# Queries and keys of the second attention and of retention projected with columns in the rows, their rotary step over partition rows with SBUF transfers and GpSimd

## The chip, the cores and the metric

The kernel runs on one core of a Trainium2 chip. A core has five engines that work side by side and meet through semaphores: TensorE (PE) multiplies matrices and transposes, VectorE (DVE) and ScalarE (ACT) work elementwise on SBUF and PSUM, GpSimd (POOL) does elementwise work on SBUF, and SyncE (SP) issues transfers. The metric is the device time of one execution in microseconds (us), lower is better. Before the change it is 839.24 us, the median of three runs between 838.96 and 839.48.

## What is computed

A decoder trunk of two layers over 256 tokens of width 1024. Each layer normalises, projects with one wide matrix `w_in`, runs three token mixers on parts of the projection, merges them behind gates, and adds a squared-ReLU MLP. Cut to what matters here:

```python
def apply_rope(x, cos, sin):
    half = x.shape[-1] // 2
    x1, x2 = x[..., :half], x[..., half:]
    return jnp.concatenate([x1 * c - x2 * s, x1 * s + x2 * c], axis=-1)

p = rms_norm(x, attn_norm[l]) @ w_in
(cq, ckv, k_rope, mq, mk, mv, rq, rk, rv, rg, g_mla, g_moba, g_ret) = split(p)
o_mla  = mla_branch(...)        # first attention, 8 heads
o_moba = moba_branch(mq, mk, mv)  # second attention, 8 heads of 64, the first 16 of each turned
o_ret  = retention_branch(rq, rk, rv, rg)  # 4 heads of 64, all 64 turned
merged = (sigmoid(g_mla) * (o_mla @ w_branch_mla)
          + sigmoid(g_moba) * (o_moba @ w_branch_moba)
          + sigmoid(g_ret) * (o_ret @ w_branch_ret))
x = x + merged @ w_out
x = x + square(relu(rms_norm(x, mlp_norm[l]) @ w_up)) @ w_down
```

With 256 tokens there is one MoBA block, so the second attention is causal attention over all tokens. In the retention, scores are multiplied by a fixed decay instead of a softmax. "Rotary step", or rope, is `apply_rope`.

## The kernel before

**Numbers.** Everything is float32. A weight block comes from memory as `raw` (up to 128 x 1024, 512 KB, on SP's queue), ACT rounds it to a high part `whi` and DVE subtracts to get the low part `wlo` (lines 191 and 193). There are 4 `raw` buffers and 6 each of `whi` and `wlo`. The normalised activations `xs` are held in the same two parts, with the channels in the partition rows and both parts side by side. A product then is three matmuls (`three`, lines 211 to 214): high by high, high by low, low by high.

**Order.** The matrix work of a layer is a list of units, `prog`; `at(slot(key, i), step)` hangs a step (transposes, scores, softmax) behind unit `i` of the projection `key`. A scheduler with due times orders the instructions of each engine within what this list, the buffers and the data allow; between `tc.manual_schedule` marks PE's order is as written. Projections run in the order b0 (the MLA's compressed q and kv), mq, mk, the MLA's own up projections between the units of mv, gmla, gmoba, bmla, rqk, rv, rg, bmoba, gret, bret, wout, and then the MLP.

**Tokens in the rows.** `project` (line 324) takes two accumulators in PSUM, one for each 128 tokens, and walks over four weight blocks of two channel groups each: 48 matmuls over 512 columns for a projection of 512. The tag `acc` has 4 banks, the tag `misc` another 4. `moba_done` and `ret_done` (lines 624 and 799) evict with an ACT copy that multiplies by the reciprocal norm of the token (`xn.col`), and for mq, mk and rqk `rope` (line 359) follows: two products and a sum and a difference on DVE.

**Turning.** The scores need channels in the rows. `moba_turn` (line 776) transposes mq and mk, 8 transposes of 128x128 for each of 4 pairs of heads into a bank `pqk`; `ret_turn` (line 812) does the same for rqk into `prt`. `copied_pair` (line 391) copies the bank to `qkT` on ACT. The scores of four heads then run together (`together`, line 381): `moba_scores` (line 785) at gmoba0's second unit and GAP = 8 units later, `ret_scores` (line 822) at rg's first unit. `in_a_row` (line 373) writes PE's order by hand for the values of the heads before and the scores of the next ones.

**The start.** In layer 0 the projections b0 and mq run together, channel group by channel group as x arrives (`start`, line 635). In layer 1 b0 runs in two turns, one for each 128 tokens, while the last MLP results of layer 0 are turned and added (`before`, line 1092). `c_norms` (line 594) then squares x, sums and calls `stats`; `xn.square` adds up on DVE in the attention norm and on GpSimd in the MLP norm.

**The MLP's up projection** (line 987) already gives channels in the rows: 8 matmuls over 512 columns with `whi` as the stationary operand and both parts of xs as the moving one, then 8 over 256 with `wlo`; lines 1010 and 1011 add the halves.

Of the kernel before, what the change touches and what calls it, by code (L numbers as in the profile page):

```python
# [14 lines left out]
P = 128  # L15
D = 1024
S = 256
# [17 lines left out]
C_MQ, C_MK, C_MV = range(416, 928), range(928, 1440), range(1440, 1952)  # L35
# [7 lines left out]
]  # L43
C_KV = [P * h + o + i for o in (0, NOPE) for h in range(MLA_H) for i in range(64)]


def weight_plan():

    plan = []

    def block(key, name, kt, cols, per):
        for j in range(0, kt, per):
            plan.append(((*key, j // per), name, (j, per), cols))

    def span(c, n):
        return range(c, c + n)

    for l in range(L):
        if l == 0:

            for i in range(2):
                plan.append(((l, "mq", i), "w_in", (0, 1), span(C_MQ.start + 256 * i, 256)))
            plan.append(((l, "b0", 0), "w_in", (0, 1), C_MLA))
            for k in range(1, KD):
                plan.append(((l, "b0mq", k), "w_in", (k, 1), range(0, 928)))
# [50 lines left out]
K_COS_RT = K_SIN_MB + NT * 8  # L116
K_SIN_RT = K_COS_RT + NT * 32
K_DEC = K_SIN_RT + NT * 32
K_END = K_DEC + RT_H * 3 * P

# [8 lines left out]
def trunk(ctx: ExitStack, tc: tile.TileContext, gx, wts, consts, gfin, gn, xtok, out):  # L129
# [16 lines left out]
    DEC = cp.tile([P, K_END - K_DEC], F32, name="DEC")  # L146
# [90 lines left out]
    class Normed:  # L237


        def __init__(self, g0, adds=nc.vector):  # L240
            self.g0, self.adds = g0, adds
            self.parts = [t4(f"xs{i}").rearrange("p (k two) s -> p k two s", two=2) for i in range(KD // 2)]
            self.sums = []
# [12 lines left out]
        def square(self, n):  # L256
            if n == 0:
                self.sum = sb.tile([P, S], F32, name="sqsum", bufs=1)
                nc.scalar.activation(self.sum, chunk(n), AF.Square)
            else:  # L260
                sq = sb.tile([P, S], F32, name="xsq", bufs=2)
                nc.scalar.activation(sq, chunk(n), AF.Square)
                self.adds.tensor_add(self.sum, self.sum, sq)
# [94 lines left out]

    def rope(xv, c0, s0, t, n, h, w=None):

        w = w or n
        cos = K[:, c0 + t * w : c0 + t * w + n][:, None, None, :].to_broadcast([P, h, 2, n])
        sin = K[:, s0 + t * w : s0 + t * w + n][:, None, None, :].to_broadcast([P, h, 2, n])
        a = sb.tile([P, 512], F32, name="ropea", bufs=1)
        b = sb.tile([P, 512], F32, name="ropeb", bufs=1)
        av = a[:, : 2 * h * n].rearrange("p (h two n) -> p h two n", h=h, two=2)
        bv = b[:, : 2 * h * n].rearrange("p (h two n) -> p h two n", h=h, two=2)
        nc.vector.tensor_mul(av, xv, cos)
        nc.vector.tensor_mul(bv, xv, sin)
        nc.vector.tensor_sub(xv[:, :, 0, :], av[:, :, 0, :], bv[:, :, 1, :])  # L370
        nc.vector.tensor_add(xv[:, :, 1, :], av[:, :, 1, :], bv[:, :, 0, :])
# [18 lines left out]

    def copied_pair(pt):

        o = sb.tile([P, 2 * S], F32, name="qkT", bufs=4)
        nc.scalar.copy(o, pt)
        return o[:, 0:S], o[:, S:]
# [150 lines left out]
    xn = Normed(G_ATT)  # L546
# [11 lines left out]
    begin((0, "mk", 0))  # L558
# [28 lines left out]
    def layer(l, xn, before):  # L587
# [36 lines left out]
        def moba_done(key):  # L624
            def done(accs):
                dst = mqkv[key] = [w2k(key) for _ in range(NT)]
                for t in range(NT):
                    nc.scalar.activation(dst[t], accs[t], AF.Copy, scale=xn.col[t])
                    if key != "mv":
                        xv = dst[t].rearrange("p (h d) -> p h d", h=MB_H)[:, :, 0:16]  # L630
                        rope(xv.rearrange("p h (two n) -> p h two n", two=2), K_COS_MB, K_SIN_MB, t, 8, MB_H)
# [30 lines left out]

        if l:
            project(l, "mq", xn, 512, moba_done("mq"))
# [9 lines left out]
        project(l, "mk", xn, 512, moba_done("mk"))  # L674
# [82 lines left out]
        if l == 0:  # L757
            at(slot("gmla1", 0), lambda: tc.keep_in_program_order(nc.sync.dma_start(DEC, consts[:, K_DEC:])))
# [13 lines left out]
        first = slot("gmoba0", 1)  # L772
        at(first, lambda: omobaT.extend((t4("omobah"), t4("omobal"))))
        qkT = {}

        def moba_turn(i):
            pt = misc_tile("pqk")
            for a, key in enumerate(("mq", "mk")):
                for t in range(NT):
                    nc.tensor.transpose(  # L780
                        pt[:, (2 * a + t) * P : (2 * a + t + 1) * P], mqkv[key][t][:, P * i : P * i + P], ident
                    )
            qkT[i] = copied_pair(pt)

        def moba_scores(h0):
# [3 lines left out]
                [(banks[2 * i : 2 * i + 2], *qkT[h0 // 2 + i]) for i in range(2)],  # L789
# [3 lines left out]
        for i in range(4):  # L793
            at(first + 4 * (i // 2) - 3 + i % 2, lambda i=i: moba_turn(i))
# [4 lines left out]
        def ret_done(key):  # L799
            def done(accs):  # L800
                dst = rqkv[key] = [w2k(key) for _ in range(NT)]
                for t in range(NT):
                    nc.scalar.activation(dst[t], accs[t], AF.Copy, scale=xn.col[t])
                    if key == "rqk":
                        xv = dst[t].rearrange("p (h two n) -> p h two n", h=2 * RT_H, two=2)
                        rope(xv, K_COS_RT, K_SIN_RT, t, 32, 2 * RT_H)

            return done

        rT, or_ps, aT, rg, oret = [], [], {}, {}, []  # L810

        def ret_turn(i):
            pt = misc_tile("prt")
            for a in range(2):
                for t in range(NT):
                    nc.tensor.transpose(
                        pt[:, (2 * a + t) * P : (2 * a + t + 1) * P],
                        rqkv["rqk"][t][:, 256 * a + P * i : 256 * a + P * i + P], ident,
                    )
            rT.append(copied_pair(pt))  # L820

        def ret_scores():
# [3 lines left out]
                [(banks[2 * i : 2 * i + 2], rT[i][1], rT[i][0]) for i in (1, 0)],  # L826
# [58 lines left out]
        project(l, "rqk", xn, 512, ret_done("rqk"))  # L885
# [43 lines left out]
        for i in range(2):  # L929
            at(slot("rv", 1 + i), lambda i=i: ret_turn(i))  # L930
# [35 lines left out]
        def wout_first():  # L966
            xm.append(Normed(G_MLP + KD * l, nc.gpsimd))
# [101 lines left out]
        if not last:  # L1069
            xn = Normed(G_ATT + KD * (l + 1))  # L1070
# [83 lines left out]
def constants():  # L1154
# [14 lines left out]
    for c, s, dim, theta in (  # L1169
        (K_COS_MLA, K_SIN_MLA, ROPE, 500000.0),  # L1170
        (K_COS_MB, K_SIN_MB, MB_D // 4, 500000.0),
        (K_COS_RT, K_SIN_RT, RT_K, 10000.0),
    ):
        n = dim // 2
        inv = f(1.0) / (f(theta) ** (np.arange(0, dim, 2, dtype=f) / f(dim)))
        ang = np.arange(S, dtype=f)[:, None] * inv[None, :].astype(f)
        two = 2 if c == K_COS_MLA else 1
        w = two * n
        for t in range(NT):
            K[:, c + t * w : c + t * w + w] = np.tile(np.cos(ang[P * t : P * t + P]), two)  # L1180
            K[:, s + t * w : s + t * w + w] = np.tile(np.sin(ang[P * t : P * t + P]), two)
    return K
# [44 lines left out]
```

## Time and profile before

| | before |
|---|---|
| Device time, median of 3 runs | 839.24 us (838.96 to 839.48) |
| Profiled execution, its own time | 839.34 us |
| Its span, first to last instruction | 837.5 us |
| Granted TensorE clock, mean | 0.999 |
| Queries and keys transposed, `pqk` and `prt` | 32 and 16 transposes |
| Transfers on SP's queue | 151 MB in all, mean 180 GB/s |

The times come from runs without the profiler; the profile describes one further execution, whose span is 1.8 us shorter than its own time. An engine's busy time is the union of its instructions; PE's matmuls are pipelined, so records overlap, and a matmul's length is more than what it adds. In a row of groups stand line, engine, operation, names and shapes, count, then the duration (least, median and most in ns, and first and last start) or the busy time and mean. "idle before <-releaser" is the time that the engine waited just before and what ended the wait.

### The profile page before, as it was taken

Reading aid. Unit: us, or ns where it says so; the run is one execution under the profiler, and the core shown is the slowest. Engines: PE = TensorE matmul, PEld = TensorE weight load, DVE = VectorE, ACT = ScalarE, POOL = GpSimd, SP = SyncE. Lnnn points to the kernel's source line nnn. Section 1 sums busy time; section 2 is a strip of 40 time slices with the busy share of each in tenths; the row PEclk is TensorE's granted clock in tenths of the full one; section 3 lists DMA queues with packets and bytes.
Section 4 is the critical chain, followed back from the end, with each engine's and each line's share of the span. In section 5 each row is a group of like instructions: output and inputs, shape, how many; then the busy total and the mean of one; then the engine's idle time right before and its main releaser. Section 6 shows DMA issues by size and latency. Waiting matters only on the chain.

```text
span 837.5 us, 11975 instructions
## 1 busy us (share of the span) xinstructions
PE 830.7 (99%) x4342; PEld 702.9 (84%) x4342; DVE 577.0 (69%) x1088; ACT 490.0 (59%) x860; POOL 42.0 (5%) x45
## 2 busy tenths in 40 slices
PE   9999999999999999999999999999999999999997
PEld 7888788888888888888888888888888888888886
DVE  6887567595787666656589765766968775556663
ACT  7857566445555555555677576744555555555552
POOL 0100000040030000000000000001201200000000
PEclk9999999999999999999999999999999999999999
DMA  9865454536456656666367544564565666666641
GB/s 345 271 201 188 144 166 146 175 125 213 141 180 228 193 193 189 195 187 189 114 202 223 173 143 151 151 182 149 157 199 163 213 179 193 199 189 192 196 129 51
DMA packets 43115, 151.09 MB, mean 180 GB/s; under 512 B 4912, under 2 KB 5936, under 8 KB 43056
## 3 DMA queue, kind: packets, MB, share of 16 engines
q1 hardware_dynamic: 42480, 149.66, 56.7%
q8 instruction: 34, 0.56, 0.3%
q10 hardware_dynamic: 576, 0.67, 0.2%
q14 instruction: 25, 0.20, 0.1%
HBM read 149.26 MB, written 1.05 MB: 179 GB/s over the span
## 4 chain that ended last, share of the span: by engine, by line
PE 99%; ACT 0%; DVE 0%; issue 0%; DVEq 0%
PE acc L212 20%; PE acc L213 20%; PE acc L214 20%; PE pup L1002 13%; PE pup L1004 7%; PE acc L952 5%; PE ps_s L763 1%; PE ps_pt L429 1%; PE po L456 1%; PE ps_s L389 1%; PE acc L656 1%; PE acc L657 0%; PE acc L659 0%; PE warm L567 0%; PE po L458 0%; PE pqk L780 0%
## 5 line engine op out<-in xcount | busy, mean ns | idle before, releaser
L193 DVE TENSOR_TENSOR wlo<-raw,whi 128x1024 fp32r<-128x1024 f32 (+4 forms) x287 | 339.2, 1188 | 205.8 <-ACT whi L191 152.1
L191 ACT ACTIVATE whi<-raw 128x1024 fp32r<-128x1024 f32 (+4 forms) x287 | 292.0, 1023 | 178.8 <-PE acc L214 101.9
L212 PE MATMUL acc<-whi,xs 128*128 128x512 f32 (+1 forms) x384 | 152.0, 398 | 0.0
L213 PE MATMUL acc<-wlo,xs 128*128 128x512 f32 (+1 forms) x384 | 150.6, 392 | 0.0
L214 PE MATMUL acc<-whi,xs 128*128 128x512 f32 (+1 forms) x384 | 150.1, 392 | 0.0
L1002 PE MATMUL pup<-xs,whi 128*128 128x512 f32 x496 | 121.5, 390 | 0.0
L1002 PEld LDWEIGHTS pup<-xs,whi 128*128 128x128 f32 x496 | 91.9, 188 | 18.3
L212 PE MATMUL acc<-whi,sq 128*128 128x512 f32 x256 | 100.1, 391 | 0.0
L213 PE MATMUL acc<-wlo,sq 128*128 128x512 f32 x256 | 99.9, 390 | 0.0
L214 PE MATMUL acc<-whi,sq 128*128 128x512 f32 x256 | 98.8, 389 | 0.0
L214 PEld LDWEIGHTS acc<-whi,xs 128*128 128x128 f32 x384 | 72.1, 188 | 14.3
L212 PEld LDWEIGHTS acc<-whi,xs 128*128 128x128 f32 x384 | 72.1, 188 | 14.2 <-issue 0.7
L213 PEld LDWEIGHTS acc<-wlo,xs 128*128 128x128 f32 x384 | 72.2, 188 | 13.7 <-issue 0.3
L1004 PE MATMUL pup<-xs,wlo 128*128 128x256 f32 x496 | 68.8, 283 | 0.0
L1004 PEld LDWEIGHTS pup<-xs,wlo 128*128 128x128 f32 x496 | 65.7, 191 | 3.1
L1013 ACT ACTIVATE relu<-relu 128x256 f32<-128x256 f32 x64 | 25.5, 408 | 54.1 <-DVE relu L1012 54.1
L214 PEld LDWEIGHTS acc<-whi,sq 128*128 128x128 f32 x256 | 48.1, 188 | 10.2
L212 PEld LDWEIGHTS acc<-whi,sq 128*128 128x128 f32 x256 | 48.2, 188 | 9.2
L213 PEld LDWEIGHTS acc<-wlo,sq 128*128 128x128 f32 x256 | 48.2, 188 | 8.9
L418 ACT ACTIVATE prob<-prob,smx 128x128 f32<-128x128 f32 x64 | 28.4, 445 | 20.1 <-DVE smx L415 20.0
L952 PE MATMUL acc<-mT,whi 128*128 128x512 f32 (+1 forms) x144 | 35.3, 372 | 0.0
L1010 ACT COPY relu<-pup 128x256 f32<-128x256 f32 x62 | 22.3, 365 | 16.0 <-PE pup L1004 15.2
(246 smaller groups left out, 1006.0 us busy)
## 6 DMA issues: line engine op xcount, KB each, us to landing
raw<-wts SPq DMA_DIRECT2D x264, 512.0 KB, 4.1
raw<-wts SPq DMA_DIRECT2D x6, 464.0 KB, 8.0
raw<-wts SPq DMA_DIRECT2D x4, 416.0 KB, 3.3
xrow<-xtok SPq DMA_DIRECT2D x4, 256.0 KB, 8.0
gn<-gn SPq DMA_DIRECT2D x2, 512.0 KB, 4.7
raw<-wts SPq DMA_DIRECT2D x3, 256.0 KB, 4.1
DEC<-consts SPq DMA_DIRECT2D x1, 768.0 KB, 6.0
y<-y SPq DMA_DIRECT2D x2, 352.0 KB, 2.6
```

The source lines that it names most:

```text
L191: nc.scalar.activation(hi[:, cs], raw[:, cs], AF.Copy)
L193: nc.vector.tensor_sub(lo[:, cs], raw[:, cs], hi[:, cs].bitcast(F32))
L212: nc.tensor.matmul(o, ah, bh, start=start, stop=False)
L213: nc.tensor.matmul(o, ah, bl, start=False, stop=False)
L214: nc.tensor.matmul(o, al, bh, start=False, stop=stop)
L389: nc.tensor.matmul(bank[:, o], a[rows, sa], b[rows, sb_], start=True, stop=True)
L418: nc.scalar.activation(p[:, a:b], p[:, a:b], AF.Exp, bias=m[:, 2 + i : 3 + i], scale=scale, accum_out=m[:, 4 + i : 5 + i])
L952: nc.tensor.matmul(o, a, b, start=half == 0 and i == 0, stop=4 * half + n == KD and i == len(jobs) - 1)
L1002: nc.tensor.matmul(u, w, xm.both(k), start=k == 0, stop=False)
L1004: nc.tensor.matmul(u[:, 0:S], w, xm.k(k)[0], start=False, stop=k == KD - 1)
L1010: nc.scalar.copy(s, u[:, S : 2 * S])
L1013: nc.scalar.activation(s, s, AF.Square)
```

## The change

mq (in layer 1), mk and rqk are projected like the MLP's up projection, so that channels lie in the rows without a transpose. Each is four units of 128 columns (`project_turned`), each with one accumulator bank and one weight block; pairs of units make a tile `qkraw` of 128 x 512. It is not multiplied by the norm: the rope's tables are (`tables`, on GpSimd). The rope then needs the other half of each head, which lies in other partition rows. `rope_turned` fetches it with four transfers of 32 x 512 from `qkraw` to `qkoth` on SP's queue, and makes two products and a sum; in MoBA all of it on GpSimd, in the retention one product on GpSimd and the rest on DVE. The columns of mq and mk are put in such an order that the turned 16 of each head lie in rows that a transfer of 32 rows exchanges. In layer 0 mq stays with tokens in the rows and is transposed, four banks' worth reduced to two.

The joint MoBA scores and all that hangs on them move from the second unit of gmoba0 to that of gmoba1, four units later. In layer 1 three of the seven additions of squares (n = 1 to 3) are done by GpSimd. The tables come with one more transfer of 512 KB (`TAB`) in layer 0; the constants `K` are 128 columns shorter.

```diff
+    def turned(key, cols):
+        for n in range(4):
+            block((*key, n), "w_in", KD, cols[P * n : P * n + P], KD)
...
             block((l, "b0"), "w_in", KD, C_MLA, 2)
-            block((l, "mq"), "w_in", KD, C_MQ, 2)
-        block((l, "mk"), "w_in", KD, C_MK, 2)
+            turned((l, "mq"), C_MQ)
+        turned((l, "mk"), C_MK)
...
-        block((l, "rqk"), "w_in", KD, C_RQK, 2)
+        turned((l, "rqk"), C_RQK)
...
-                self.adds.tensor_add(self.sum, self.sum, sq)
+                (nc.gpsimd if n < self.on_pool else nc.vector).tensor_add(self.sum, self.sum, sq)
...
+    def project_turned(l, key, xn, done):
+        pair = []
+        def unit(n):
+            wh, wl = load_w(l, key, n, 0)
+            acc = acc_tile()
+            for k in range(KD):
+                nc.tensor.matmul(acc, wh[:, k, :], xn.both(k), start=k == 0, stop=False)
+            for k in range(KD):
+                nc.tensor.matmul(acc[:, 0:S], wl[:, k, :], xn.k(k)[0], start=False, stop=k == KD - 1)
+            if n % 2 == 0:
+                pair.append(w2k("qkraw"))
+            second = sb.tile([P, S], F32, name="second", tag="relu", bufs=3)
+            nc.scalar.copy(second, acc[:, S : 2 * S])
+            nc.vector.tensor_add(halves(pair[-1])[:, n % 2, :], acc[:, 0:S], second)
+            if n % 2:
+                done(n // 2, pair[-1])
+        for n in range(4):
+            prog.append(((key, n), lambda n=n: unit(n)))
+
+    def tables(xn, kind):
+        o = sb.tile([P, 2 * S], F32, name="tab", bufs=1)
+        for i in range(2):
+            cs = slice((2 * kind + i) * S, (2 * kind + i) * S + S)
+            nc.gpsimd.tensor_mul(o[:, S * i : S * i + S], TAB[:, cs], xn.row)
+        return o
+
+    def rope_turned(raw, tab, engine):
+        other = w2k("qkoth")
+        for quarter in range(4):
+            a, b = 32 * quarter, 32 * (quarter ^ 1)
+            nc.sync.dma_start(other[a : a + 32, :], raw[b : b + 32, :])
+        o = sb.tile([P, 2 * S], F32, name="qkT", bufs=4)
+        cos, sin = (tab[:, S * i : S * i + S][:, None, :].to_broadcast([P, 2, S]) for i in range(2))
+        engine.tensor_mul(halves(o), halves(raw), cos)
+        nc.gpsimd.tensor_mul(halves(other), halves(other), sin)
+        engine.tensor_add(o, o, other)
+        return halves(o)
...
+        def moba_rope(key, i):
+            if "tab" not in mqkv:
+                mqkv["tab"] = tables(xn, 0)
+            qkT[key][i] = rope_turned(mqkv[key, i], mqkv["tab"], nc.gpsimd)
...
+        for i in range(2):
+            if l:
+                at(slot("mk", 1 + 2 * i), lambda i=i: moba_rope("mq", i))
+            at(slot("gmla0", 1 + 2 * i), lambda i=i: moba_rope("mk", i))
...
-        first = slot("gmoba0", 1)
+        first = slot("gmoba1", 1)
...
-        for i in range(4):
-            at(first + 4 * (i // 2) - 3 + i % 2, lambda i=i: moba_turn(i))
+        if l == 0:
+            for i in range(2):
+                at(first + 4 * i - 3, lambda i=i: moba_turn(i))
...
+        def ret_pair(i, raw):
+            if i == 0:
+                rqkv["tab"] = tables(xn, 1)
+            rT.append(rope_turned(raw, rqkv["tab"], nc.vector))
...
-        project(l, "rqk", xn, 512, ret_done("rqk"))
+        project_turned(l, "rqk", xn, ret_pair)
...
-        for i in range(2):
-            at(slot("rv", 1 + i), lambda i=i: ret_turn(i))
...
-            xm.append(Normed(G_MLP + KD * l, nc.gpsimd))
+            xm.append(Normed(G_MLP + KD * l, KD))
...
-            xn = Normed(G_ATT + KD * (l + 1))
+            xn = Normed(G_ATT + KD * (l + 1), 4)
```

More of the change, by code (lines that the diff above doesn't have):

```diff
@@ L34 @@
 C_MLA = range(0, 416)
[L35 removed]
+C_MV = range(1440, 1952)
 C_RQK, C_RV, C_RG = range(1952, 2464), range(2464, 2976), 2976
@@ L43 @@
 ]
+C_MQ, C_MK = (
+    [c + 64 * h + i for h in range(8) for i in (*range(8), *range(16, 40), *range(8, 16), *range(40, 64))] for c in (416, 928)
+)
 C_KV = [P * h + o + i for o in (0, NOPE) for h in range(MLA_H) for i in range(64)]
@@ L363, in rope @@
         sin = K[:, s0 + t * w : s0 + t * w + n][:, None, None, :].to_broadcast([P, h, 2, n])
-        a = sb.tile([P, 512], F32, name="ropea", bufs=1)
-        b = sb.tile([P, 512], F32, name="ropeb", bufs=1)
+        a = sb.tile([P, S], F32, name="ropea", bufs=1)
+        b = sb.tile([P, S], F32, name="ropeb", bufs=1)
         av = a[:, : 2 * h * n].rearrange("p (h two n) -> p h two n", h=h, two=2)
@@ L661, in start, with moba_pair, done @@
                 moba_done("mq")(mq)
+        qkT = {"mq": {}, "mk": {}}
+        def moba_pair(key):
+            def done(i, raw):
+                mqkv[key, i] = raw
+            return done
+        def moba_rope(key, i):
+            if "tab" not in mqkv:
+                mqkv["tab"] = tables(xn, 0)
+            qkT[key][i] = rope_turned(mqkv[key, i], mqkv["tab"], nc.gpsimd)
         if l:
-            project(l, "mq", xn, 512, moba_done("mq"))
+            project_turned(l, "mq", xn, moba_pair("mq"))
             at(slot("mq", 1), c_norms)
@@ L771, in layer @@
         branch(l, "bmla", omlaT, th_mla, merged)
-        first = slot("gmoba0", 1)
+        first = slot("gmoba1", 1)
         at(first, lambda: omobaT.extend((t4("omobah"), t4("omobal"))))
-        qkT = {}
         def moba_turn(i):
-            pt = misc_tile("pqk")
-            for a, key in enumerate(("mq", "mk")):
+            pt = misc_tile("pq")
+            for a in range(2):
                 for t in range(NT):
+                    k = 2 * i + a
                     nc.tensor.transpose(
-                        pt[:, (2 * a + t) * P : (2 * a + t + 1) * P], mqkv[key][t][:, P * i : P * i + P], ident
+                        pt[:, (2 * a + t) * P : (2 * a + t + 1) * P], mqkv["mq"][t][:, P * k : P * k + P], ident
                     )
-            qkT[i] = copied_pair(pt)
+            o = sb.tile([P, 2 * S], F32, name="qkT", bufs=4)
+            nc.scalar.copy(o, pt)
+            qkT["mq"][i] = halves(o)
         def moba_scores(h0):
@@ L788, in moba_scores @@
                 ((slice(0, P), slice(0, P), slice(0, P)), (slice(P, 3 * P), slice(P, S), slice(0, S))),
-                [(banks[2 * i : 2 * i + 2], *qkT[h0 // 2 + i]) for i in range(2)],
+                [(banks[2 * i : 2 * i + 2], *(qkT[key][h0 // 4][:, i, :] for key in ("mq", "mk"))) for i in range(2)],
             )
             return banks
-        for i in range(4):
-            at(first + 4 * (i // 2) - 3 + i % 2, lambda i=i: moba_turn(i))
+        if l == 0:
+            for i in range(2):
+                at(first + 4 * i - 3, lambda i=i: moba_turn(i))
         moba_last = attention(omobaT, None, lambda: mqkv["mv"], MB_D**-0.5, first, moba_scores, mla_last)
@@ L825, in ret_scores @@
                 ((slice(0, S), slice(0, P), slice(0, S)), (slice(S, 3 * P), slice(P, S), slice(P, S))),
-                [(banks[2 * i : 2 * i + 2], rT[i][1], rT[i][0]) for i in (1, 0)],
+                [(banks[2 * i : 2 * i + 2], rT[1][:, i, :], rT[0][:, i, :]) for i in (1, 0)],
             )
@@ L1181, in constants @@
             K[:, s + t * w : s + t * w + w] = np.tile(np.sin(ang[P * t : P * t + P]), two)
+    for j, (dim, theta) in enumerate(((MB_D // 4, 500000.0), (RT_K, 10000.0))):
+        ang = angles(dim, theta).T
+        n = dim // 2
+        c = K_TURNED + 2 * S * j
+        K[:, c : c + S] = 1.0
+        for quarter in range(4):
+            rows = slice(32 * quarter, 32 * quarter + n)
+            K[rows, c : c + S] = np.cos(ang)
+            K[rows, c + S : c + 2 * S] = np.sin(ang) * (1 if quarter % 2 else -1)
     return K
```

63 lines of the change are left out of this document (22 added, 41 removed).

## The prediction, made before the changed kernel was run

> **What bounds the kernel now.** I read the busy times of the engines first, then the chain of waits, then the windows by stage.
>
> ```profile
> PE 830.7 (99%) x4342; PEld 702.9 (84%) x4342; DVE 577.0 (69%) x1088; ACT 490.0 (59%) x860; POOL 42.0 (5%) x45
> ...
> PE 99%; ACT 0%; DVE 0%; issue 0%; DVEq 0%
> ```
>
> TensorE is busy for 830.7 of 837.5 us, and the chain that ended last lies on it for 99%. The windows (microseconds; busy time and count of PE, of its weight loads, of DVE, ACT and POOL; granted clock; DMA share; GB/s) show where the missing 6.8 us are:
>
> ```profile
> 0.00:40.00 40.00, 39.23 (x180) 32.53 (x181) 29.81 (x75) 31.44 (x61) 3.54 (x12) 1.00 0.88 311
> ...
> 450.00:480.00 30.00, 30.00 (x163) 25.81 (x162) 25.45 (x54) 19.32 (x31) 0.00 (x0) 1.00 0.57 178
> ...
> 820.00:837.50 17.50, 11.61 (x54) 9.37 (x53) 5.35 (x11) 4.76 (x13) 1.10 (x2) 0.94 0.15 60
> ```
>
> At the start 0.77 us are lost and at the end 5.89; between them PE hardly stops, and the clock is granted in full. The change touches neither end. So between the ends only two things count: what PE's own instructions cost, and whether anything new makes PE wait. DVE, at 25.45 of 30 us early in the second layer, is the engine with the least room behind it.
>
> **The price of PE's instructions.** The length of a matmul's record isn't its price, since records overlap; the price is the distance from one to the next, which the chain of waits gives as the time of a run:
>
> ```profile
> 90.67 0.44 PE pqk L780 x4
> ...
> 153.41 0.66 PE prt L816 x6
> ...
> 278.74 0.23 PE acc L214
> 278.97 3.63 PE pup L1002 x16
> 282.60 1.91 PE pup L1004 x16
> ...
> 418.00 0.19 PE acc L212
> ```
>
> A transpose of 128x128 costs 0.44/4 = 0.11 us, a matmul over 512 columns 3.63/16 = 0.227, one over 256 columns 1.91/16 = 0.119, one over 416 columns 0.19.
>
> **What goes.** The transposes of mq, mk and rqk:
>
> ```profile
> L780 PE MATMUL pqk<-K,mq x16: 270/272/273, 90.5 to 520.7; 128*128 128x128 f32 x16
> ...
> L780 PE MATMUL pqk<-K,mk x16: 272/272/273, 90.7 to 520.9; 128*128 128x128 f32 x16
> ...
> L816 PE MATMUL prt<-K,rqk x16: 270/272/273, 148.9 to 567.0; 128*128 128x128 f32 x16
> ```
>
> These are 48. Eight remain: layer 0 makes mq with tokens in the rows as before, and its turn, now called pq, takes 2 banks of 4. Forty at 0.11 us are -4.4 us on the path.
>
> **What PE pays for it.** A projection of 512 columns now costs 48 matmuls over 512 columns, 48 x 0.227 = 10.90 us. Turned, each of four units has 8 over 512 columns (the high weights with both parts of xs side by side) and 8 over 256 (the low weights): 32 x 0.227 + 32 x 0.119 = 11.08 us. That is the same form as the MLP's up projection, lines 1002 and 1004, whose rows I use. Five projections change (mk and rqk of layer 0, mq, mk and rqk of layer 1): 5 x 0.18 = +0.9 us. The scores have the same shapes as before. Without a new wait the sum is -3.5 us.
>
> **Work on the other engines.**
>
> ```profile
> L394 ACT COPY qkT<-pqk x8: 558/578/595, 91.1 to 523.3; 128x512 f32<-128x512 f32 x8
> ...
> L1010 ACT COPY relu<-pup x62: 346/364/377, 248.1 to 817.9; 128x256 f32<-128x256 f32 x62
> L1011 DVE TENSOR_TENSOR relu<-pup,relu x62: 414/418/425, 249.5 to 818.3; 128x256 f32<-128x256 f32 x62
> ...
> L368 DVE TENSOR_TENSOR ropea<-rqk,K x4: 685/689/693, 142.3 to 558.7; 128x512 f32<-128x512 f32 x4
> ...
> L370 DVE TENSOR_TENSOR rqk<-ropea,ropeb x4: 418/422/426, 143.6 to 561.0; 128x256 f32<-128x256 f32 x4
> ...
> L803 ACT ACTIVATE rqk<-acc,ms x4: 690/690/692, 141.6 to 555.5; 128x512 f32<-128x512 f32 x4
> ...
> L263 POOL TENSOR_TENSOR sqsum<-sqsum,xsq 128x256 f32<-128x256 f32 x14 | 16.0, 1142 | 117.3 <-ACT xsq L262 117.2
> L895 POOL TENSOR_TENSOR rgb<-rg,gn 128x512 f32<-128x512 f32 x4 | 5.1, 1284 | 273.4 <-DVE rg L894 273.4
> ```
>
> Each turned unit is evicted by an ACT copy (0.364) and a DVE add (0.418), 20 of each: 7.3 and 8.4 us. ACT loses ten evictions of 0.69 and ten qkT copies of 0.578, 12.7 us; DVE loses rqk's rope, 4 x (2 x 0.689 + 2 x 0.422) = 8.9 us, and the shorter ropes of mq and mk, and gains 8 operations of 0.689 for retention's turned rope. Neither has more work in sum than now; only their order can cost PE something. GpSimd's part is new: for each of 6 MoBA pairs two products and a sum over 512 columns, for each of 4 retention pairs one product, 22 at 1.28 us by the rgb row, and 8 table products of 256 columns and three additions of layer 1's squares at 1.14 (DVE does the latter in 0.42). That is some 40 us over both layers; for MoBA the cover is the distance from projection to scores, tens of microseconds, and the joint rows move from gmoba0's second unit to gmoba1's. I put them at nothing.
>
> The 40 transfers stand in SP's queue among the weights, so each delays the blocks behind it by its issue, and those by what it waits for itself.
>
> ```profile
> 171.46 0.33 SPq L176 DMA_DIRECT2D raw<-wts  x1
> ```
>
> ```profile
> L193 DVE TENSOR_TENSOR wlo<-raw,whi 128x1024 fp32r<-128x1024 f32 (+4 forms) x287 | 339.2, 1188 | 205.8 <-ACT whi L191 152.1
> L191 ACT ACTIVATE whi<-raw 128x1024 fp32r<-128x1024 f32 (+4 forms) x287 | 292.0, 1023 | 178.8 <-PE acc L214 101.9
> ```
>
> ACT and DVE split weights ahead of PE and idle because PE still holds the six buffers (101.9 us of ACT's idle time). A block lasts PE 12 x 0.227 = 2.73 us, so in the steady stages they are three to five blocks ahead, 8 to 14 us. Four issues, 4 x 0.33 = 1.3 us, vanish in that. If the cover were gone, as at a stage where blocks arrive just in time, ten groups of 1.3 us would be 13 us.
>
> **Where I expect a new wait: the start of layer 1.** Timeline of before there:
>
> ```profile
> 423.19 0.63 PE L212 MATMUL acc<-whi,xs 128*128 128x512 f32 x2
> ...
> 425.30 3.06 DVE L263 TENSOR_TENSOR sqsum<-sqsum,xsq 128x256 f32<-128x256 f32 x6
> 429.16 4.63 DVE L193 TENSOR_TENSOR wlo<-raw,whi 128x1024 fp32r<-128x1024 f32 x4 [0.79 <-ACT whi L191]
> ...
> 434.97 1.06 ACT L191 ACTIVATE whi<-raw 128x1024 fp32r<-128x1024 f32 x1 [2.45 <-DMA raw<-wts]
> ```
>
> Transfers (KB each, median us from issue to landing):
>
> ```profile
> raw<-wts SPq DMA_DIRECT2D x264, 512.0 KB, 4.1
> ...
> GX<-gx SPq DMA_DIRECT2D x1, 11.0 KB, 6.2
> ```
>
> The projections have four acc banks. In the changed order b0's two halves hold two of them until the statistics, mq's units 0 and 1 the others, and unit 2 must wait until unit 0's bank is evicted. From 423.19 PE has 24 matmuls over 416 columns (4.56) and 13 of unit 0 and unit 1's high part (2.95), then unit 0's low part (0.95): 431.65. Unit 1's last three high and its low ones take it to 433.3, the sums of squares to 433.5. Unit 0's eviction stands on ACT behind the high part of the third mk block, and its DVE add behind the low part. That block's buffer comes free when mq's third block is split, which waits for b0's first whi buffer (PE, near 424.8) and for ACT: some 426.4 to 427.7 us on DVE. A transfer then lands 4.1 us later, near 432 (the 2.45 us that ACT idles before 434.97 is this same kind of wait). whi to 433.0, the copy to 433.4, wlo (4.63/4 = 1.16) to 434.3, the add to 434.7: PE stands from 433.5 to 434.7, 1.2 us. Bounds: none if the block lands by 430.8; 2.4 us if one wlo more (1.16) gets in ahead of the add. I take 1.2, by the landing that is the median of 264 such blocks.
>
> The next bank (unit 1's) comes about 1 us before PE asks. In layer 0 the evictions of mk lie before no such queue.
>
> **The sum** for the profiled execution: 839.34 (span 837.5, 1.8 around it) - 4.4 + 0.9 + 1.2 = 837.0 us; it stood 0.1 above the median of the three runs, which changes nothing at this size.
>
> **Retention, the tightest new chain.** From the end of rqk's second unit (T), DVE's add comes at T+1.2 to T+1.7 after a wlo block. SP issues four transfers until T+3.0; a weight block is issued just ahead of them. At 4.1 us they land by T+7.1, GpSimd's product ends at T+8.4, DVE's sum at T+9.1. This sum stands in the middle of the second MoBA group's softmax on DVE, which today runs like this, first maximum to last scaling:
>
> ```profile
> 124.27 0.28 DVE L409 CUSTOM_DVE_ANT_0 prob<-ps_s,K 128x128 f32<-128x128 f32 x1
> ...
> 129.43 0.55 DVE L423 TENSOR_SCALAR prob<-prob,smx 128x128 f32<-128x128 f32 x2
> ```
>
> The second head's scaling, queued behind the sum, ends by T+9.7; PE transposes that head at T+10.4 (1.9 for values and scores, 2 x 2.77 for units 2 and 3, 2.73 for rv's first unit, 0.33). Pair 1 is evicted by about T+14, lands by T+19.2, is summed by T+21.2 and used at T+22.3. So both waits just miss PE, by 0.7 and 1.1 us; every microsecond of landing beyond about 5 is paid, in each layer. I take nothing for it.
>
> **Rivals.**
> (1) No bank wait: the third mk block lands early. For: ACT has slack there. Against: the 2.45 us idle. 839.3 - 3.5 = 835.8.
> (2) GpSimd gets in DVE's way. Its reads beside DVE's:
>
> ```profile
> 169.07 1.28 POOL L895 TENSOR_TENSOR rgb<-rg,gn 128x512 f32<-128x512 f32 x1 [133.02 <-DVE rg L894]
> ...
> 169.30 2.13 DVE L193 TENSOR_TENSOR wlo<-raw,whi 128x1024 fp32r<-128x1024 f32 x1 [0.36 <-ACT whi L191]
> 170.43 2.16 POOL L896 TENSOR_TENSOR rg<-rg,gn 128x512 f32<-128x512 f32 x1
> ```
>
> A wlo that takes 1.16 to 1.23 us took 2.13 here, 0.9 more, and the next GpSimd product 2.16 for 1.28. Layer 1 puts 12 such products (4 pairs x 3) between 445 and 490; at 0.9 each DVE loses up to 10.8 us where its idle time is 4.55 of 30, against 8 to 14 us of slack. Up to 2.5 us would reach PE: about 837 to 839.5, nearest to 838.5. The Trainium skill has a rule for it (SBUF — State Buffer, "Who interferes with whom"): a Vector instruction with two SBUF inputs and a GpSimd instruction that reads SBUF take turns at a shared port, the later one blocked until the earlier ends. The rows agree: the wlo ends 1.08 us after the first product, as if begun then. By that rule alone a product could cost DVE its whole 1.28 us, 15.4 for the twelve, and this rival would end near 840.
> (3) Slower: the small transfers queue behind weight blocks. Place: retention in both layers. If the last lands 6.2 us after its issue (the 11 KB row, taken where DMA is 88% busy; here it is about 55%), pair 0's sum ends at T+11.2 and the second head is 1.4 late; pair 1 then follows some 1.9 late. About 3 us a layer: 837.0 + 6 = 843. It costs from 5 us of landing on, and eats the gain from about 5.8 on.
> (4) The change doesn't shorten PE at all, if 256-column matmuls cost more than 0.119 in this order. The pup row, with the same loads and shapes, speaks against it.
>
> **How the numbers follow.** The forecast with its neighbourhood (836.3 to 838) has 0.42, rival 1 0.15, rival 2 0.23, rival 3 0.18, rival 4 0.02. What a measurement of this kernel can tell from no change is 0.2%, 1.7 us: faster is below 837.56, slower above 840.92. Faster takes nearly all of rival 1, most of the forecast's part and a little of rival 2: 0.58. Same takes the forecast's upper tail and most of rival 2: 0.22. Slower: rival 3 and the end of rival 2: 0.20. The likeliest case alone ranges from 835.8 to 838.5; the range for 8 in 10 goes from 835.4 to 842, taking in the lower half of rival 3.
>
> **What would show it.** PE's busy time falls by about 3.5 us to 827, with 40 fewer transposes. In the chain of waits one break of 1 to 2 us near 433, released by DVE's add. No break at the joint scores of MoBA. The transfers of 64 KB land in 3 to 5 us; above 5 the retention scores or the transposes of the second head show PE idle. A wlo beside GpSimd's products lasts 2 us. Wrong would be: PE idle spread over 445 to 490 (rival 2), or a busy time of PE that doesn't fall.

## The result, and the profile after

| | before | after |
|---|---|---|
| Device time, median of 22 runs | 839.17 us (838.80 to 839.69) | 837.92 us (837.43 to 839.04) |
| Ratio of after to before | | 0.9986 (95% interval 0.9980 to 0.9993) |
| Profiled execution, its own time | 839.34 us | 837.58 us |
| Its span | 837.5 us | 835.8 us |

The change takes 1.25 us away, 0.14%: a gain whose interval leaves out 1, and which is smaller than the 0.2% that the prediction called measurable. The profiled execution gained 1.76 us; it lies 0.34 below its own median.

The page after the change, busy times and shares of the chain:

```profile
PE 827.3 (99%) x4382; PEld 702.7 (84%) x4382; DVE 588.5 (70%) x1073; ACT 483.8 (58%) x860; POOL 84.1 (10%) x78
...
PE 97%; DVE 1%; DMA 1%; issue 0%; ACT 0%; DVEq 0%; ACTq 0%
```

PE works 3.4 us less. The chain no longer lies on it alone: DVE and a transfer have 1% each, so something new makes PE wait. What PE waited for (total us, times, longest):

```profile
PE acc L377 <- DVE qkraw L384: 1.2, 1, 1.2
PE warm L615 <- PEq L1286: 0.8, 1, 0.8
PE acc L222 <- DVE xs L236: 0.4, 1, 0.4
```

The second is the start, as before. The other two are new: 3.4 less work and 1.6 more waiting make the 1.7 us of the span. Both lie at the start of layer 1, as the windows show (columns as in the prediction):

```profile
400.00:430.00 30.00, 29.61 (x166) 26.46 (x165) 22.26 (x40) 21.35 (x43) 2.44 (x3) 1.00 0.47 150
430.00:450.00 20.00, 18.75 (x114) 16.64 (x113) 16.68 (x39) 12.74 (x29) 11.16 (x10) 1.00 0.76 227
450.00:480.00 30.00, 30.00 (x167) 26.05 (x165) 28.94 (x46) 18.02 (x30) 10.46 (x6) 1.00 0.58 179
```

PE stands 0.39 us before 430 and 1.25 after it, and nowhere else between start and end. DVE, at 25.45 of 30 us before, is now at 28.94 with 46 instructions for 54: fewer, and each longer.

The chain of waits after the change, in order of time (start us, us, what), shows the longer wait whole:

```profile
426.13 0.10 DVE sqsum L272
426.23 4.49 DMA raw<-wts
...
430.81 1.07 ACT whi L199
...
431.89 0.32 DVE wlo L201
...
433.04 0.43 DVE qkraw L384
433.47 0.04 issue
433.51 2.11 PE acc L377 x8
```

This is the path of the prediction: a weight block whose buffer came free at 426.2, 4.49 us of transfer, the high part on ACT, the low part on DVE, and behind it in DVE's queue the add that frees mq's first bank. PE starts the third unit at 433.51, 1.2 us late.

The shorter wait was not predicted. GpSimd's and DVE's timelines in the changed kernel:

```profile
420.87 2.66 POOL L272 TENSOR_TENSOR sqsum<-sqsum,xsq 128x256 f32<-128x256 f32 x3 [172.37 <-issue]
```

```profile
421.04 2.64 DVE L236 SCALAR_TENSOR_TENSOR xs<-GX,xs 128x128 fp32r<-128x128 f32 x4
423.61 1.13 DVE L236 SCALAR_TENSOR_TENSOR xs<-x,GX,xs 128x128 fp32r<-128x128 f32 x4
```

Before, DVE's four instructions took 1.13 us, as the next four still do:

```profile
422.86 1.13 DVE L228 SCALAR_TENSOR_TENSOR xs<-GX,xs 128x128 fp32r<-128x128 f32 x4
```

Beside GpSimd's three additions of squares they took 2.64 and ended at 423.68, 0.15 us after those. PE waited for their result.

### The profile page after: what moved, and what is told of

It is laid out like the page before. It is cut to its first block, busy times and chain, and to the rows that moved or that the text cites. A ratio compares the mean times of both kernels' runs of the same rounds, so it can differ in the third digit from the quotient of the medians.

```text
span 835.8 us, 12166 instructions
## 1 busy us (share of the span) xinstructions
PE 827.3 (99%) x4382; PEld 702.7 (84%) x4382; DVE 588.5 (70%) x1073; ACT 483.8 (58%) x860; POOL 84.1 (10%) x78
## 4 chain that ended last, share of the span: by engine, by line
PE 97%; DVE 1%; DMA 1%; issue 0%; ACT 0%; DVEq 0%; ACTq 0%
PE acc L220 18%; PE acc L222 18%; PE acc L221 18%; PE pup L1062 14%; PE pup L1064 7%; PE acc L1012 5%; PE acc L377 4%; PE acc L379 2%; PE ps_pt L477 1%; PE ps_s L829 1%; PE po L504 1%; PE ps_s L443 1%; DMA raw<-wts 1%; DVE wlo L201 1%; PE acc L704 0%; DVE xs L236 0%
## 5 line engine op out<-in xcount | busy, mean ns | idle before, releaser
L220 PE MATMUL acc<-whi,xs 128*128 128x512 f32 (+1 forms) x304 | 120.2, 395 | 0.0
L222 PE MATMUL acc<-whi,xs 128*128 128x512 f32 (+1 forms) x304 | 118.5, 391 | 0.4 <-DVE xs L236 0.4
L221 PE MATMUL acc<-wlo,xs 128*128 128x512 f32 (+1 forms) x304 | 118.8, 391 | 0.0
L222 PEld LDWEIGHTS acc<-whi,xs 128*128 128x128 f32 x304 | 57.1, 188 | 12.4 <-DVE xs L236 0.7
L220 PEld LDWEIGHTS acc<-whi,xs 128*128 128x128 f32 x304 | 57.1, 188 | 11.5 <-issue 0.7
L221 PEld LDWEIGHTS acc<-wlo,xs 128*128 128x128 f32 x304 | 57.2, 188 | 10.7
L272 POOL TENSOR_TENSOR sqsum<-sqsum,xsq 128x256 f32<-128x256 f32 x17 | 18.4, 1085 | 289.9 <-issue 172.4
L377 PE MATMUL acc<-xs,whi 128*128 128x512 f32 x160 | 41.3, 395 | 1.2 <-DVE qkraw L384 1.2
```

Of the source, the lines that this page charges most:

```text
L220: nc.tensor.matmul(o, ah, bh, start=start, stop=False)
L221: nc.tensor.matmul(o, ah, bl, start=False, stop=False)
L222: nc.tensor.matmul(o, al, bh, start=False, stop=stop)
L272: (nc.gpsimd if n < self.on_pool else nc.vector).tensor_add(self.sum, self.sum, sq)
L377: nc.tensor.matmul(acc, wh[:, k, :], xn.both(k), start=k == 0, stop=False)
```

## The experiments

All are edits of the changed kernel. The times are medians; "after" stands for 837.92.

**Three additions back on DVE.**

```diff
-            xn = Normed(G_ATT + KD * (l + 1), 4)
+            xn = Normed(G_ATT + KD * (l + 1), 0)
```

> The three additions of squares at layer 1's start go back to DVE (on_pool 4 -> 0), nothing else is edited. Theory A (in the changed kernel GpSimd's additions block DVE's xs, four of which took 2.64 us for 1.13, and PE waits 0.4 us for xs): the four xs take about 1.1 us again, PE's wait for xs is gone, and the time falls by 0.3 to 0.6 us, from 837.9 to about 837.4; the bank wait of 1.2 us stays. Rival B (the xs would have come late anyway, behind DVE's own queue): the wait of 0.4 stays, no change. Rival C (three additions more on DVE, 1.3 us, push the weights and the eviction of mq's first unit back): the bank wait grows to about 2 us, 838.3.

838.03 us (837.61 to 838.47), ratio to before 0.9987 (0.9978 to 0.9996): no change. The four xs and PE's waits:

```profile
421.39 1.13 DVE L236 SCALAR_TENSOR_TENSOR xs<-GX,xs 128x128 fp32r<-128x128 f32 x4
```

```profile
PE pqr L803 <- DVE qr L425: 0.6, 1, 0.6
PE acc L377 <- DVE qkraw L384: 0.6, 1, 0.6
PE b L704 <- ACT whi L199: 0.2, 1, 0.2
```

The cause of the shorter wait is as theory A has it: without GpSimd's additions the xs take 1.13 us and PE doesn't wait for them. The time is not. The bank wait is 0.6 here, and at 462.87 there is a new wait of 0.6 for the rope of the first attention's queries (qr). Whether the edit brought these two isn't shown: the bank wait also differs between two executions of the unedited kernel (last experiment).

**b0 in the other four banks.**

```diff
-project(l, "b0", xn, 416, b0.extend, before, ((0,), (1,)))
+project(l, "b0", xn, 416, b0.extend, before, ((0,), (1,)), misc_tile)
```

> In layer 1 b0's two accumulators come from the misc banks, so mq's four units have four acc banks. Theory A (the wait of 1.2 us before mq's third unit is for a bank alone): PE doesn't stop there, the wait for xs of 0.4 stays, 836.7. Rival B (the bank hides another wait behind it, for the weights of the third unit or for the statistics): PE stops there all the same, 0.5 us or more, 837.3 to 837.9. Rival C: the misc banks are now short, and the transposes of the compressed q and kv wait, 838 or more.

837.18 us (836.80 to 838.23), ratio 0.9977 (0.9969 to 0.9986), profiled execution 836.86. The only wait left behind the start is the one for xs:

```profile
PE misc L222 <- DVE xs L236: 0.4, 1, 0.4
```

So the longer wait was for a bank and hid no other wait behind it, as theory A says. It is worth 0.74 us by the medians and 0.72 by the profiled executions, less than the 1.2 of the first profile.

**Both edits.**

> Both edits: additions of squares on DVE and b0 in the misc banks. Theory A (the two waits are all that the changed kernel loses against its PE sum): PE's busy time stays at 827.3, no wait is left between the start and the end, 836.3. Rival B (some of the loss lies elsewhere, as the median of the changed kernel is 0.35 above its profiled run): 836.7 or more with waits spread out in the profile.

836.93 us (836.50 to 837.72), ratio 0.9974 (0.9964 to 0.9984); the profiled execution took 836.53. PE is busy for 827.8 us and waits for nothing but the start. Against before that is 2.2 us by the medians. Theory A is right about the waits. The median lies 0.6 us above its 836.3, as rival B has it, but without rival B's waits: in the profile PE is busy for 0.5 us more than after the change.

**Layer 1's mq with tokens in the rows.**

```diff
-            turned((l, "mq"), C_MQ)
+            block((l, "mq"), "w_in", KD, C_MQ, 2)
...
-            project_turned(l, "mq", xn, moba_pair("mq"))
+            project(l, "mq", xn, 512, moba_done("mq"))
```

> Layer 1's mq is projected with tokens in the rows and turned by eight transposes, as layer 0's; mk and rqk stay as changed. Theory A: PE's busy time rises by 8 x 0.11 - 0.18 = 0.7 us to 828.0, both waits at layer 1's start are gone, since the token-major form has work on the first 128 tokens while xs of the second half comes and needs no third bank: 837.9 + 0.7 - 1.6 = 837.0, less than the whole change. Rival B (the loss doesn't hang on mq's turned form): 838.6.

837.06 us (836.59 to 837.26), ratio 0.9974 (0.9964 to 0.9985), as theory A says. PE does more (827.8 us) and waits at layer 1's start for nothing. In the changed kernel's order, turning this one of the five projections cost more than it brought.

**No transfers.** The ropes read their own rows in place of the partner's.

```diff
-        for quarter in range(4):
-            a, b = 32 * quarter, 32 * (quarter ^ 1)
-            nc.sync.dma_start(other[a : a + 32, :], raw[b : b + 32, :])
...
-        nc.gpsimd.tensor_mul(halves(other), halves(other), sin)
+        nc.gpsimd.tensor_mul(halves(other), halves(raw), sin)
```

> Leaves the 40 transfers of 64 KB out: the second product of each rope reads qkraw itself, so the rope adds each row's own value for its partner's and the scores are others. Theory A (transfers and their 0.6 us issues on SP are hidden everywhere; the retention chain just misses PE): 837.9 within 0.3, both waits at layer 1's start still there. Rival B (the transfers delay weight blocks or the retention's scores in some executions, which is why the median lies 0.35 above the profiled run): about 837.5 and a narrower spread.

850.81 us (848.76 to 851.04), ratio 1.0132 (1.0115 to 1.0149): 13 us slower for less work, against both theories. What PE waited for, and the window behind layer 1's start:

```profile
PE pqr L800 <- DVE qr L422: 7.5, 3, 4.7
```

```profile
450.00:480.00 30.00, 25.32 (x139) 22.30 (x138) 29.03 (x32) 14.63 (x23) 21.03 (x13) 0.89 0.45 141
```

GpSimd no longer waits for transfers and runs its rope operations one behind the other, 21.03 of 30 us. DVE is busy for 29.03 us and gets 32 instructions through, where the changed kernel has 46. Two instructions of DVE's timeline:

```profile
469.11 1.48 DVE L420 TENSOR_TENSOR ropeb<-qr,K 128x256 f32<-128x256 f32 x1
...
472.18 0.81 DVE L421 TENSOR_TENSOR qr<-ropea,ropeb 128x128 f32<-128x128 f32 x1
```

Alone they take 0.42 and 0.29. The transfers had spaced GpSimd's work.

The waits are not the whole loss. PE waited for 8.1 us more than after the change, and it was busy for 5.1 us more (832.4). A lower granted clock accounts for most of that: behind PE's waits of 2.38 and 4.68 us for qr it was 0.50 from 57 to 59 and from 473 to 479 us, while waits of 1.25 us (after the change, clock from 433 to 435) and 1.77 us (the experiment with the joint rows below, clock from 100 to 105) left it at 1.00.

**No transfers, and the ropes on DVE.** As the last one, all three operations on DVE.

> As e5 without the 40 transfers (each row's own value stands for its partner's, so the scores are others), but all three operations of every rope on DVE, so that GpSimd only makes the tables and layer 1's three additions. Theory A (e5 lost 13 us because GpSimd's rope operations, no longer spaced by transfers, blocked DVE where its qr rope was due): the wait of pqr for qr falls from 7.5 us to under 1, DVE's busy time is below e5's 598 although it has 22 operations of 0.69 (15 us) more, and the time is 837.5 to 839. Rival B (e5 was slow because the order of the work was another, transfers or not): 845 or more again.

839.59 us (838.34 to 841.40), ratio 1.0005 (0.9996 to 1.0014); the profiled execution took 838.34. The wait for qr is gone, DVE's busy time is 590.5 for the last one's 598.2 with 15 us more work of its own, and 11 of the 13 us are back. So what slowed the last kernel was GpSimd's operations beside DVE's, theory A, and not its order. The median lies above the range of theory A; that the runs spread over 3 us was expected by neither.

**MoBA's first product and sum on DVE.**

```diff
-            qkT[key][i] = rope_turned(mqkv[key, i], mqkv["tab"], nc.gpsimd)
+            qkT[key][i] = rope_turned(mqkv[key, i], mqkv["tab"], nc.vector)
```

> MoBA's first product and sum go to DVE (12 operations of 0.69 us), only the second product stays on GpSimd. Theory A (GpSimd's operations cost DVE as much by blocking as they would on DVE, DVE's busy time having risen by 11.5 us though its work fell by about 2): DVE's busy time rises by less than 4 us against the changed kernel's 588.5, PE's waits stay as they are, 837.9 within 0.4. Rival B (blocking is cheap, DVE takes the full 8.3 us more, of which 4 to 5 between 442 and 480): DVE about 597 and the time 838.5 or more. Rival C: blocking is what widens the runs; a narrower spread and 837.6.

839.04 us (837.54 to 841.70), ratio 1.0001 (0.9990 to 1.0011): the gain is lost. DVE is busy for 586.0 us, 2.5 less than after the change, although it does 12 x 0.69 = 8.3 us more. So GpSimd's 12 operations had cost DVE 8.3 + 2.5 = 10.8 us, 0.9 each: more than the 0.69 that DVE takes to do one itself. Theory A is right there and wrong in the time, and this is why:

```profile
44.23 1.80 DVE L408 TENSOR_TENSOR qkT<-qkraw,tab 128x512 f32<-128x512 f32 x2 [3.43 <-POOL tab L396]
```

DVE's queue now holds products that wait for GpSimd's tables, here 3.43 us, and all that is queued behind them waits too: the first attention's compressed parts (cTl) and keys (KK) in layer 0, 0.8 and 0.4 us of PE's time. GpSimd itself had stood 6.01 us for the transfer of TAB before it made these tables. In this kernel GpSimd's operations blocked DVE in short pieces, and a wait in DVE's own queue blocked it whole. Rival C fails: the runs spread over 4.2 us, after the change over 1.6.

**Each rope's transfers twice.** Four transfers of 32x464 into an unread tile come first.

> Each rope first makes four transfers of 32x464 into a tile that nobody reads, then its own four, so its own land at least 2.3 us later (four issues of 0.58). Theory A (in the changed kernel the second head's scaling is 1.7 to 2.0 us ahead of PE, and the retention's scores 0.9 us, in each layer): the second head comes 0.3 to 0.7 late; pair 1's transfers start 2.3 later and land another 2.3 later, so the scores come 3 to 3.5 late: 3.5 to 4 us a layer, 845 to 846. MoBA's part stays hidden. Rival B (margins are larger than the profile says, or transfers overlap so that four more cost little): below 840.

839.43 us (838.52 to 841.04), ratio 1.0004 (0.9995 to 1.0013): 1.5 us slower, rival B. PE waits nowhere in the retention. The instructions' order had moved: pair 0's sum stood behind the last of the four heads' scalings on DVE, and no longer between the first and the second:

```profile
141.44 0.55 DVE L475 TENSOR_SCALAR prob<-prob,smx 128x128 f32<-128x128 f32 x2
143.19 0.69 DVE L414 TENSOR_TENSOR qkT<-qkT,qkoth 128x512 f32<-128x512 f32 x1 [1.20 <-POOL qkoth L413]
```

So nothing of the softmax waited for it. The retention's scores had moved too, to 158.39, 2 us further behind the softmax's last transposes than after the change. The experiment therefore doesn't tell what a later landing would cost in the changed kernel's order. The profiled execution (839.64) took 2.1 us more than the changed kernel's. Of these, 0.8 are waits elsewhere, for qr (0.5) and for the first attention's keys (0.3); for the other 1.3 PE was busy, and no cause of that is shown.

**Joint rows four units earlier.**

```diff
-        first = slot("gmoba1", 1)
+        first = slot("gmoba0", 1)
```

> The joint MoBA scores and what hangs on them go back to gmoba0's second unit. Theory A (the ropes are done by 493 us in layer 1 and PE's sum is the same in either place): 837.9 within 0.4. Rival B (the scores then come while GpSimd's last ropes of mk and the first attention's softmax hold DVE, and PE waits for scores or probabilities): 838.5 to 840 with waits at ps_s or ps_pt in the profile.

839.92 us (839.04 to 840.22), ratio 1.0006 (0.9997 to 1.0015): 2.0 us slower, rival B in size but at another place:

```profile
101.25 0.65 PE L504 MATMUL po<-probT,vml 128*64 128x256 f32 x4 [1.77 <-ACT probT L479]
```

The joint rows begin with the values of the first attention's last heads, and those heads' probabilities aren't turned yet in layer 0. Moving the row, which the prediction put at nothing, is worth 2 us.

**Both edits, and mq's ropes later.** As the third experiment, with `at(slot("gmla0", 2 * i), ...)` for mq's ropes of layer 1.

> As e3 (additions on DVE, b0 in the misc banks), and mq's ropes of layer 1 at gmla0's first and third unit instead of mk's second and fourth, so that GpSimd's 12 rope operations lie behind the qr rope. Theory A (what is left between median and profiled run in e3, 0.4 us, are executions in which GpSimd's ropes delay DVE between 442 and 460): DVE's busy time in 450 to 480 falls from about 28.5 towards 26, the median comes to 836.5 and the runs lie within 0.7 us. Rival B (the scatter comes from the transfers' landing or from before that): 836.9 and a spread of 1.2 us as in e3. Rival C (12 rope operations in a row now collide with the first attention's softmax): slower, 838.

837.07 us (836.52 to 837.97), ratio 0.9975 (0.9965 to 0.9986): rival B. DVE is busy for 27.04 us in 450 to 480, where it was 28.36 in the third experiment, without effect on the median. The profiled execution (837.69) waited in layer 0, which the edit doesn't touch: 0.6 us for a whi and 0.5 for KK.

**mq with tokens in the rows, additions on DVE.**

> As e4 (layer 1's mq with tokens in the rows), and the additions of squares on DVE. Theory A (with mq in rows PE has no wait at layer 1's start, so nothing is to be won there; the additions only load DVE): 837.0 as e4, within 0.2. Rival B (GpSimd's additions still cost something hidden): 836.6.

836.85 us (836.54 to 837.67), ratio 0.9973 (0.9962 to 0.9984). That is 0.2 us below the experiment with mq alone, between theory A's 837.0 and rival B's 836.6 and a little nearer to A; the runs don't decide. This and the third experiment are the fastest versions, 2.3 us under before, and can't be told apart. So even without waits turning layer 1's mq brought nothing that shows: PE is busy for 827.8 us with it and 827.9 without, where the prices of the prediction make a difference of 0.7.

**The changed kernel once more.**

> The changed kernel once more, unedited, for a second profiled execution. Its 22 runs spread over 1.6 us (before: 0.9) and its profiled run was 0.35 below the median. Theory A (the scatter comes from layer 0, where e8, e9 and e10 showed waits of 0.3 to 0.6 us for the split of a weight block near 25 us and for the first attention's keys near 50): an execution near or above the median shows one of these beside the two waits of layer 1 (1.2 and 0.4). Rival B (the scatter is the length of the bank wait itself, which hangs on a transfer's landing): only the bank wait differs from 1.2.

838.11 us (837.28 to 838.64), ratio 0.9987 (0.9977 to 0.9996). Its profiled execution took 837.45:

```profile
PE acc L222 <- DVE xs L236: 0.4, 1, 0.4
PE acc L377 <- DVE qkraw L384: 0.2, 1, 0.2
PE acc L220 <- DVE KK L774: 0.2, 1, 0.2
```

Both theories hold in part. The bank wait varies, 0.2 us here and 1.2 in the first profile, and a wait in layer 0 comes and goes. PE was busy for 0.6 us more, so the total hardly differs. Both profiled executions of the changed kernel lay below their medians (by 0.34 and 0.66 us), but that of MoBA's products on DVE lay 0.64 above its own. A profile shows one execution out of this scatter; what makes the scatter stays open.

## Why the prediction was right, point by point

- **What goes and what PE pays.** Forecast -4.4 and +0.9, in all -3.5; PE's busy time fell by 3.4, and by 2.9 and 2.8 in the edit without waits and in the changed kernel's second profile. So the sum held within 0.7 us. In the chain after the change 8 of the turned matmuls over 512 columns take 1.84 us (at 436.58) and 8 over 256 take 0.95 (at 435.62): 0.230 and 0.119 each. Rival 4 is out.
- **The bank wait.** Forecast 1.2 us, from 433.5 to 434.7, by an add behind a block landing near 432. It was 1.2 us in the first profile, on that path step by step, ending at 433.51; both ends lay 1.2 us earlier than forecast on before's clock, since PE came to the last transposes of layer 0's results 1.8 us earlier (418.29 for 420.11) and then lost 0.4 to xs. Removing the need for the bank removed the wait. But that the size came out to a tenth was luck: over the eight profiles with the turned mq and with b0 in the acc banks the wait was 0.2, 0.5, 0.6, 0.8, 1.0 and three times 1.2, so the forecast hit the top of its range.
- **The size.** 837.0 was forecast for the profiled execution, which took 837.58: -1.76 us where -2.3 was forecast. The medians differ by -1.25. The prediction gave 0.58 to a time below 837.56, and 837.92 lies above it, so the outcome that it held likeliest didn't come. The step that failed is the one that put GpSimd's new work at nothing. Its additions of squares cost PE 0.4 us through DVE's xs: the wait stands in all eight profiles in which GpSimd makes these additions and mq is turned, and in none of the three with them on DVE. That is the wait alone; taking only the additions away left the time where it was (838.03). Together with the 0.1 us that PE's work fell short, it makes up nearly all of the profiled execution's 0.58. Another 0.34 us lies between it and the median and isn't explained.
- **GpSimd in DVE's way (rival 2).** The mechanism and its price of 0.9 us an operation were right. The 10.8 us measured are for another twelve operations than the prediction's, so that the totals agree is chance. DVE's own instructions came to some 2 us less work, as the prediction says, and yet its busy time rose by 11.5 us: the prediction's count of the work left out what GpSimd's operations add to it. In the first profile none of it reached PE between 445 and 490, as the forecast took it; in two of the experiments a wait of 0.5 to 0.6 us for qr stands there (462.87 and 464.89). The time of 837.92 lies in rival 2's range, 837 to 839.5, as well as in the forecast's, 836.3 to 838, so the number alone doesn't choose between them; the waits in the profile do. And it is the danger of this kernel: without the spacing that the transfers give it lost 13 us, the lower clock included, of which 11 came back with the ropes on DVE.
- **The retention's chain.** Transfers landed in 4.8 us (4.1 taken) and took 0.58 us each to issue (0.33 taken), so that four took 2.4 us and not 1.3:

```profile
qkoth<-qkraw SPq DMA_DIRECT2D x40, 64.0 KB, 4.8
```

```profile
140.41 0.54 DVE L471 TENSOR_SCALAR prob<-prob,smx 128x128 f32<-128x128 f32 x2
...
153.31 0.69 DVE L410 TENSOR_TENSOR qkT<-qkT,qkoth 128x512 f32<-128x512 f32 x1 [4.81 <-POOL qkoth L409]
```

```profile
142.58 0.82 PE L477 MATMUL ps_pt<-K,prob 128*128 128x128 f32 x6
...
154.92 1.36 PE L443 MATMUL ps_r<-qkT 64*128 64x256 f32 x12
```

  These are of layer 0. The second head's scaling ended at 140.95, and PE took it up three transposes into the row that begins at 142.58: some 2 us of margin, not 0.7 (the prediction's own terms add up to T+10.5, a margin of 0.8). Pair 1's sum ended at 154.00 for 154.92: 0.9, forecast 1.1. In layer 1 the margins were 1.7 and 0.9. Rival 3 didn't come about.
- **The joint rows.** That PE would show no break there was right, and it was the moved row that made it so: in the old place the break is 1.8 us.

## What to carry to other kernels

In this kernel work taken off the bound engine came back as a wait at the one place where the others had no lead, the start of a layer, where two banks were still held. Look for such a place first, and ask whether the moved part is needed there at all. GpSimd, busy for 10% of the time, wasn't free: price what such an engine's operations cost a neighbour by their number and spacing, not by its busy share. And before taking a wait or a transfer away, ask what it keeps apart.

## What the runs showed of the hardware that wasn't expected

GpSimd's and DVE's operations on two SBUF inputs took turns: four xs of 1.13 us took 2.64 beside 2.66 us of GpSimd, and a wlo of 1.22 us took 2.00 in the changed kernel:

```profile
442.49 3.53 POOL L408 TENSOR_TENSOR qkT<-qkraw,tab 128x512 f32<-128x512 f32 x2
```

```profile
442.87 2.00 DVE L201 TENSOR_TENSOR wlo<-raw,whi 128x1024 fp32r<-128x1024 f32 x1
...
450.51 1.78 DVE L758 COPY KK<-krT 64x1024 f32<-64x1024 f32 x1
```

The Trainium skill (SBUF — State Buffer, "Who interferes with whom") says that the later of two such instructions is blocked until the earlier ends, and the traces agree: the wlo ends at 444.87, 1.1 us after the first product would have ended alone (442.49 + 1.28), about what a wlo takes by itself. The copy of one input in the last line, 0.69 us alone, took 1.78 beside a GpSimd sum as well. The traces show what it does to a queue. GpSimd's operations lengthen too (3.53 us for two of 1.28), and in the experiment without transfers a run of them kept DVE busy for 29.03 of 30 us with 32 instructions for 46.

Small SBUF transfers weren't quicker than large ones on the same queue. 64 KB landed in 4.8 us, the median of 40, and 512 KB in 4.2, the median of 264 over the whole run. In the four stretches where both occur (50 to 80, 130 to 150, 440 to 470 and 550 to 566 us) the medians are 5.3, 4.6, 4.8 and 4.9 for 64 KB and 4.6, 5.4, 4.4 and 5.9 for 512 KB. On SP each small one took 0.58 us to issue, a weight block 0.33.
